# The delta rule of a hybrid layer: 16x16 substitution blocks with one more level of products, and the sample's chunk padded to 128 tokens

## The chip, the cores and the metric

The kernel runs on one core of a Trainium2 chip. The metric is the device time of one execution in microseconds (us). The core has five engines that work side by side, each on a queue of its own that it runs in order: PE (TensorE, matrix products), DVE (VectorE), ACT (ScalarE), POOL (GpSimd) and SP (SyncE), which here only issues DMA transfers. An engine whose next instruction waits for a semaphore does nothing that is queued behind it.

## What is computed

One layer of a streaming encoder: a projection of the normed input, then two branches, a gated delta rule over 16 heads and a sparse attention, then two output projections. There are 512 prompt tokens and 64 sample tokens (T = 576). The change is in the delta rule. Cut to what matters, for each head:

```
A  = where(strict, (k * beta) @ k.T * decay, 0)          # within a chunk
Tm = triangular_solve(eye + A, eye)                       # inverse of a unit lower triangle
u, w = Tm @ (v * beta), Tm @ (k * beta * exp(gc))
qk = (q @ k.T) * decay
def step(S, ...):                                         # one chunk after the other
    v_new = u_i - w_i @ S
    o_i   = qd_i @ S + qk_i @ v_new
    S     = S * g_last + kd_i.T @ v_new
```

The kernel takes chunks of 128 tokens for the prompt (chunks 0 to 3) and one of 64 for the sample (chunk 4), which starts from a state of its own.

## The kernel before

**The stream.** All projections run as one stream of products `mm` on PE: 128 weight columns against 288 tokens, weights and input split in a high and a low part, so that a tile of 128 columns takes 3 x 16 x 2 = 96 products. `half` issues them, `split` makes the two parts of the next tile's weights (`whi`, `wlo`), `load` fetches raw weights (`wraw`) on SP's queue. A head of the delta rule has about four and a quarter tiles of the stream beside it: its q, k and v columns, and others that it shares the stage with.

**The planner.** Everything else is a set of generator tasks. After each stream product `tick` steps the tasks that are due. A task yields what it waits for; the planner (class `Plan`) keeps its own estimate of when each buffer is ready, with fixed costs for each engine and for DMAs, and a task is due when that estimate says so. So the order of every engine's queue is fixed when the program is built, by estimates; on the chip semaphores make each instruction wait for what it really needs. `take` and `drop` are locks: only one head at a time is in `solve` (the lock "solve"), and only one in `scan`.

**A head.** `conv` makes q, k and v; `decays` the two decay matrices `QK` and `N` (tiles named e1 and e2, `e` in the trace). `front_k` multiplies k with itself (`within`, products kk, the sample's part apart as kk6s in head 6), scales `N` and starts `solve`; `front_q` does the same for q (kq). `tokens` turns k and v into token order (`kd`, `vb`).

**solve** inverts the unit lower triangles of the five chunks. It stores `N` to DRAM (`dN`), gathers the 18 diagonal blocks of 32x32 into `M`, one block a partition, and runs 30 substitution steps of two DVE operations each (a product into `Mt`, a sum into `M`). A transposed copy `X` goes beside it. Both are stored (`dX`) and loaded back by ten transfers to the diagonal blocks of `TT` (the transposed inverse) and `T1`. Products then join blocks: z0 and z1 from 32 to 64, y0 and y1 from 64 to 128:

```
self.mm(o, N[R, at:at + 32], TT[R, at + 32:at + 64], tile_position=(b + 32, b))                  # z0
self.mm(o, T1[b:b + 32, 64 * t:64 * t + 32], Z[b:b + 32, t, :], tile_position=(b, b))             # z1
```

**scan** takes the chunks in the order 0, 1, 4, 2, 3. In each: `pks` = K S and `po` = Q S on PE, `r` on DVE, `px` = TT r on PE, `x` on ACT, `pS` = kd x and `po` += QK x on PE, the new `S` on DVE. For the sample all of these are 64 tokens wide. At the end `oTp` and `oTq` transpose the head's output. All operations but those of PE are recorded by one helper, so they have one line in the profile (L55); the stream and the small products have L218, the transposes L233.

## Time and profile before

| | us |
|---|---|
| median of three runs | 3089.07 |
| the three runs | 3082.39, 3091.2, 3089.07 |
| the profiled execution | 3076.14 |
| its span | 3074.4 |
| PE busy | 2949.8 (96%) |
| DVE busy | 1389.5 (45%) |
| ACT busy | 1542.1 (50%) |
| POOL busy | 390.6 (13%) |

The profiled execution is one more run of the same kernel, recorded by the hardware; all rows below are from it. Its time is a little above its span, which goes from the first recorded instruction to the last. Busy time of PE counts overlapping products once. The 16 heads of the delta rule lie between about 560 and 1640 us of the span.

### The profile page before, as it was taken

The page shows a single profiled execution, that of the slowest core. Times are in us where ns is not written, and L with a number is a line of the kernel's source. Part 1 is how long each engine was busy: PE and PEld are TensorE (multiplying, and loading weights), DVE is VectorE, ACT ScalarE, POOL GpSimd, SP SyncE. Part 2 cuts the span into 40 slices and gives each one's busy share as a digit, 9 for nine tenths or more (in the row PEclk, how much of TensorE's full clock was granted, in tenths as well). Part 3 has the DMA queues.
Part 4 walks back from the last instruction along what each step waited for, and adds up shares of the span by engine and source line. Part 5 has one row for each costly group of instructions (what it writes and reads, how often), then busy time and mean ns, then how long its engine had stood idle before and what let it go on. Part 6 is the DMA issues. An engine that isn't in the chain of part 4 may idle for free.

```text
span 3074.4 us, 56422 instructions
## 1 busy us (share of the span) xinstructions
PE 2949.8 (96%) x22363; PEld 2811.9 (91%) x22363; DVE 1389.5 (45%) x4059; ACT 1542.1 (50%) x3332; POOL 390.6 (13%) x727
## 2 busy tenths in 40 slices
PE   6999999999999999999998799999999999999897
PEld 2599999999999989999997799899999999999897
DVE  3344997666567657666641344344412111111112
ACT  3266445565555556665553355445544444444454
POOL 1001111111111111111110011011111111111110
PEclk7999999999999999999998899999999999999999
DMA  9865887766666666677667767776769899888875
GB/s 327 279 157 124 196 184 178 159 154 155 142 149 145 151 146 148 148 172 161 156 151 155 163 167 171 188 171 160 174 152 250 220 240 237 215 203 223 215 161 140
DMA packets 567242, 552.40 MB, mean 180 GB/s; under 512 B 53505, under 2 KB 466066, under 8 KB 565762
## 3 DMA queue, kind: packets, MB, share of 16 engines
q1 hardware_dynamic: 512690, 351.58, 40.5%
q0 software_dynamic: 54144, 197.16, 33.7%
q8 instruction: 176, 2.88, 0.4%
q14 instruction: 88, 0.72, 0.1%
q10 hardware_dynamic: 144, 0.07, 0.0%
HBM read 303.54 MB, written 48.04 MB: 114 GB/s over the span
## 4 chain that ended last, share of the span: by engine, by line
PE 78%; DMA 11%; SPq 3%; ACT 3%; DVE 3%; issue 2%; POOL 0%; ACTq 0%; DVEq 0%; POOLq 0%
PE mm L218 63%; SPq L55 3%; DMA za<-d_za 2%; DMA wlo<-wraw 2%; DMA gbl<-d_gb 1%; PE ada L218 1%; PE ob L218 1%; DMA wa<-in_w_ada 1%; PE lg L218 1%; PE po L218 1%; PE dot L218 1%; ACT wlo L55 1%; PE mmp L218 1%; DMA xf<-in_x_sample 1%; ACT whi L55 1%
## 5 line engine op out<-in xcount | busy, mean ns | idle before, releaser
L218 PE MATMUL mm<-hh,whi 128*128 128x288 f32 (+1 forms) x4448 | 1221.0, 301 | 4.5 <-ACT gth L55 4.2
L218 PE MATMUL mm<-hl,whi 128*128 128x288 f32 (+1 forms) x4448 | 1218.3, 300 | 0.0
L218 PEld LDWEIGHTS mm<-hh,whi 128*128 128x128 f32 (+1 forms) x4448 | 839.6, 189 | 18.1 <-issue 7.8
L218 PEld LDWEIGHTS mm<-hl,whi 128*128 128x128 f32 (+1 forms) x4448 | 840.1, 189 | 10.2 <-issue 6.1
L218 PE MATMUL mm<-hh,wlo 128*128 128x288 f32 (+1 forms) x4448 | 682.5, 303 | 4.8 <-DMA wlo<-wraw 4.8
L218 PEld LDWEIGHTS mm<-hh,wlo 128*128 128x128 f32 (+1 forms) x4448 | 618.2, 191 | 11.5 <-DMA wlo<-wraw 5.1
L55 POOL DMA_DIRECT2D wlo<-wraw x376 | 324.5, 863 | 2311.4 <-ACT wlo L55 2035.2
L55 ACT ACTIVATE wlo<-whi 128x512 fp32r<-128x512 f32 x752 | 475.8, 633 | 81.1 <-PE mm L218 46.1
L55 ACT ACTIVATE whi<-wraw 128x512 fp32r<-128x512 f32 x756 | 467.9, 619 | 78.4 <-DMA wraw<-in_w_branch_b 27.5
L55 DVE TENSOR_TENSOR Mt<-M 18x30 f32<-18x30 f32 (+14 forms) x480 | 151.7, 316 | 31.2 <-DMA M<-dN 21.9
L55 DVE TENSOR_TENSOR M<-M,Mt 18x30 f32<-18x30 f32 (+14 forms) x480 | 153.6, 320 | 16.7 <-DVE Mt L55 0.3
L218 PE MATMUL mm<-ga,whi 128*128 128x288 f32 x1024 | 140.9, 297 | 6.1 <-DVE ta L55 5.0
L218 PE MATMUL mm<-mg,whi 128*128 128x288 f32 x1024 | 144.9, 299 | 0.0
L218 PEld LDWEIGHTS mm<-ga,whi 128*128 128x128 f32 x1024 | 138.2, 190 | 7.0 <-DVE ta L55 5.7
L218 PEld LDWEIGHTS mm<-mg,whi 128*128 128x128 f32 x1024 | 139.5, 190 | 0.0
L218 PE MATMUL mm<-gb,whi 128*128 128x288 f32 x1024 | 138.6, 295 | 0.0
L218 PEld LDWEIGHTS mm<-gb,whi 128*128 128x128 f32 x1024 | 136.8, 188 | 0.0
L55 DVE SCALAR_TENSOR_TENSOR cv<-raw,cw,cv 128x579 f32<-128x579 f32 x144 | 117.4, 815 | 4.3 <-ACT cv L55 0.8
L55 DVE SCALAR_TENSOR_TENSOR gacc<-gada,cs,gacc 128x512 f32<-128x512 f32 x120 | 86.7, 745 | 31.4 <-DMA gada<-in_w_ada 31.4
L55 ACT ACTIVATE x<-px 128x128 f32<-128x128 f32 (+1 forms) x80 | 22.0, 275 | 149.2 <-PE px L218 149.2
L55 ACT ACTIVATE raw<-mm 128x288 f32<-128x288 f32 x96 | 36.7, 382 | 99.0 <-PE mm L218 98.2
L55 DVE TENSOR_TENSOR xf<-yp,xf 128x512 f32<-128x512 f32 (+1 forms) x18 | 11.4, 633 | 161.9 <-PE yp L233 134.8
(478 smaller groups left out, 3298.7 us busy)
## 6 DMA issues: line engine op xcount, KB each, us to landing
wlo<-wraw POOLq DMA_DIRECT2D x376, 512.0 KB, 5.4
wraw<-in_w_in SPq DMA_DIRECT2D x140, 1024.0 KB
wa<-in_w_ada SPq DMA_DIRECT2D x64, 512.0 KB
gada<-in_w_ada SPq DMA_DIRECT2D x64, 256.0 KB
wraw<-in_w_branch_a SPq DMA_DIRECT2D x16, 1024.0 KB
wraw<-in_w_branch_b SPq DMA_DIRECT2D x16, 1024.0 KB
wraw<-in_w_out SPq DMA_DIRECT2D x16, 1024.0 KB
d_t<-gth SPq DMA_DIRECT2D x32, 288.0 KB
```

Source lines behind the costliest of these rows:

```text
L55: r = f(*a, **k)
L218: self.nc.tensor.matmul(out, lhsT, rhs, start=start, stop=stop, **k)
```

## The change

The diagonal blocks become 16x16: 36 of them in `M`, 14 substitution steps instead of 30, five gathers instead of six. `M` and `X` go to two DRAM tiles `d_D0` and `d_D1`, which are filled with zeros once before the first head; ten transfers write the blocks to their places on the diagonal (`blocks`), and two transfers load the whole tiles, `d_D1` into `TT` and `d_D0` into a new tile `Df`. Two new stages of products, u0 and u1, join blocks from 16 to 32: 18 and 31 products of 32x32, each on the diagonal 32x32 tile of PE that belongs to its partitions, with a mask `ur` in between that keeps the upper right quarter. Then z0, z1, y0 and y1 follow as before.

For the sample's chunk, q, k, kd, vb, TT and e1 get 64 further columns or rows of zeros, so that its products are 128 wide; the outputs of the added tokens are not stored. The memsets for that are on POOL. All lines behind the new ones move: L55, L218 and L233 become L58, L221 and L236.

The diff, cut to its core:

```
--- before.py
+++ after.py
...
+TXP = 643
+TC = 640
...
+        self.d_D = [dt([128, T], F32, name=f"d_D{e}") for e in range(2)]
...
-            dst = st["qk"[j]] = p.tile([128, TX], F32, tag="qk"[j], name="qk"[j] + str(h))
+            full = st["qk"[j]] = p.tile([128, TXP], F32, tag="qk"[j], name="qk"[j] + str(h))
+            G.memset(full[:, TX:], 0.0)
+            dst = full[:, :TX]
...
+        self.G.memset(dst[64:128, 4, :], 0.0)
...
-        e1 = p.tile([128, T], F32, tag="e1", name=f"e1{h}")
+        e1x = p.tile([128, TC], F32, tag="e1", name=f"e1{h}")
+        G.memset(e1x[:, T:], 0.0)
+        e1 = e1x[:, :T]
...
-            self.mm(pk[:, b:b + n] if c < 4 else ps[:n, :n], k[:, a:a + n], x[:, a:a + n])
+            self.mm(pk[:, b:b + n] if c < 4 else ps[:, :n], k[:, a:a + 128], x[:, a:a + n])
...
+    def blocks(self, d, t):
+
+        return bass.AP(tensor=d.tensor, offset=d.offset + 128 * t, ap=[[16 * T + 16, 8 if t < 4 else 4], [T, 16], [1, 16]])
+
     def solve(self, st):
 
 
         A, V, G, S, p, h, N = self.A, self.V, self.G, self.S, self.p2, st["h"], st["N"]
         if h > 1:
             yield from self.wait(self.heads[h - 2]["scan"])
-        TT = p.tile([128, T], F32, tag="TT", name=f"TT{h}")
+        TTX = p.tile([128, TC], F32, tag="TT", name=f"TT{h}")
+        TT = TTX[:, :T]
+        G.memset(TTX[:64, T:], 0.0)
+        G.memset(TTX[64:128, TP:], 0.0)
         T1 = p.tile([128, 288], F32, tag="T1", name=f"T1{h}")
         N4, TT4, T4 = by_chunk(N), by_chunk(TT), T1[:, :256].rearrange("p (a b) -> p a b", b=64)
-        for x in (TT4[32:64, :, 0:32], TT4[64:128, :, 0:64], TT4[96:128, :, 64:96], TT[32:64, TP:TP + 32], T4[0:32, :, 32:64]):
-            G.memset(x, 0.0)
+        G.memset(T4[0:32, :, 32:64], 0.0)
         yield from self.take("solve")
         yield [N]
         dN = self.dp.tile([128, T], F32, tag="dN", name=f"dN{h}", bufs=2)
         S.dma_start(dN, N)
         yield [dN]
-        MX = p.tile([128, 32, 32], F32, tag="M", name=f"M{h}", bufs=1)
-        M, X = MX[0:18], MX[64:82]
+        MX = p.tile([128, 16, 16], F32, tag="M", name=f"M{h}", bufs=1)
+        M, X = MX[0:36], MX[64:100]
+        for t in range(5):
+            S.dma_start(M[8 * t:min(8 * t + 8, 36)], self.blocks(dN, t))
+        yield [MX]
+        tmp = p.tile([36, 64], F32, tag="Mt", name=f"Mt{h}", bufs=1)
+        for j in range(1, 15):
+            n = 15 - j
+            w = [36, n, j]
+            tv = tmp[:, :n * j].rearrange("p (a b) -> p a b", b=j)
+            V.tensor_tensor(tv, M[:, j + 1:16, j:j + 1].to_broadcast(w), M[:, j:j + 1, 0:j].to_broadcast(w), op=ALU.mult)
+            V.tensor_tensor(M[:, j + 1:16, 0:j], M[:, j + 1:16, 0:j], tv, op=ALU.add)
+            yield ("dve", self.solve_gap)
+        V.memset(M.rearrange("p a b -> p (a b)")[:, 0:256:17], 1.0)
+        A.activation(X, M.rearrange("p a b -> p b a"), AF.Copy)
+        yield [MX]
+
+        for e, x in enumerate((M, X)):
+            for t in range(5):
+                S.dma_start(self.blocks(self.d_D[e], t), x[8 * t:min(8 * t + 8, 36)])
+        yield [self.d_D[0], self.d_D[1]]
+        Df = p.tile([128, T], F32, tag="Df", name=f"Df{h}", bufs=1)
+        S.dma_start(TT, self.d_D[1])
+        S.dma_start(Df, self.d_D[0])
+        D4 = by_chunk(Df)
         B = [slice(32 * b, 32 * b + 32) for b in range(4)]
-        C = [slice(TP + 32 * b, TP + 32 * b + 32) for b in range(2)]
-        for b in range(4):
-            S.dma_start(M[4 * b:4 * b + 4], by_chunk(dN)[B[b], :, B[b]].rearrange("r t c -> t r c"))
-        for b in range(2):
-            S.dma_start(M[16 + b:17 + b], dN[B[b], C[b]].unsqueeze(0))
-        yield [MX]
-        tmp = p.tile([18, 256], F32, tag="Mt", name=f"Mt{h}", bufs=1)
-        for j in range(1, 31):
-            n = 31 - j
-            w = [18, n, j]
-            tv = tmp[:, :n * j].rearrange("p (a b) -> p a b", b=j)
-            V.tensor_tensor(tv, M[:, j + 1:32, j:j + 1].to_broadcast(w), M[:, j:j + 1, 0:j].to_broadcast(w), op=ALU.mult)
-            V.tensor_tensor(M[:, j + 1:32, 0:j], M[:, j + 1:32, 0:j], tv, op=ALU.add)
-            yield ("dve", self.solve_gap)
-        V.memset(M.rearrange("p a b -> p (a b)")[:, 0:1024:33], 1.0)
-        A.activation(X, M.rearrange("p a b -> p b a"), AF.Copy)
-        dX = self.dp.tile([2, 18, 32, 32], F32, tag="dX", name=f"dX{h}", bufs=2)
-        yield [MX]
-        S.dma_start(dX[0], M)
-        S.dma_start(dX[1], X)
-        yield [dX]
-        for b in range(4):
-            S.dma_start(TT4[B[b], :, B[b]], dX[1, 4 * b:4 * b + 4].rearrange("t r c -> r t c"))
-            if b < 3:
-                S.dma_start(T4[B[b], :, B[b % 2]], dX[0, 4 * b:4 * b + 4].rearrange("t r c -> r t c"))
-        for b in range(2):
-            S.dma_start(TT[B[b], C[b]], dX[1, 16 + b])
-        S.dma_start(T1[0:32, 256:288], dX[0, 16])
-        yield [TT, T1], 3000.0
+        blk = [(t, g) for t in range(5) for g in range(4 if t < 4 else 2)]
+        yield [TT, Df], 3000.0
 
         Z = p.tile([128, 5, 32], F32, tag="Z", name=f"Z{h}", bufs=1)
+        pz = yield from self.tr(f"u0{h}")
+        for t, g in blk:
+            at = slice(128 * t + 32 * g, 128 * t + 32 * g + 32)
+            self.mm(pz[B[g], 32 * t:32 * t + 32], N[B[g], at], TT[B[g], at], tile_position=(32 * g, 32 * g))
+        V.tensor_tensor(Z[:, 0:4, :], pz[:, 0:128].rearrange("p (a b) -> p a b", b=32),
+                        self.ur.unsqueeze(1).to_broadcast([128, 4, 32]), op=ALU.mult)
+        V.tensor_tensor(Z[0:64, 4, :], pz[0:64, 128:160], self.ur[0:64], op=ALU.mult)
+        yield [Z], 300.0
+        pz = yield from self.tr(f"u1{h}")
+        for t, g in blk:
+            at = slice(128 * t + 32 * g, 128 * t + 32 * g + 32)
+            self.mm(pz[B[g], 32 * t:32 * t + 32], Df[B[g], at], Z[B[g], t, :], tile_position=(32 * g, 32 * g))
+            if g < (3 if t < 4 else 1):
+                self.mm(pz[B[g], 160 + 32 * t:192 + 32 * t], Z[B[g], t, :], Df[B[g], at], tile_position=(32 * g, 32 * g))
+        for g in range(4):
+            R, c = slice(32 * g, 32 * g + 16), 32 * g + 16
+            A.activation(TT4[R, :, c:c + 16], pz[R, 0:128].rearrange("p (a b) -> p a b", b=32)[:, :, 16:32], AF.Copy)
+            if g < 2:
+                A.activation(TT[R, TP + c:TP + c + 16], pz[R, 144:160], AF.Copy)
+            if g < 3:
+                V.tensor_tensor(T4[B[g], :, B[g % 2]], pz[B[g], 160:288].rearrange("p (a b) -> p a b", b=32), D4[B[g], :, B[g]], op=ALU.add)
+        V.tensor_tensor(T1[0:32, 256:288], pz[0:32, 288:320], Df[0:32, TP:TP + 32], op=ALU.add)
+        yield [TT, T1], 300.0
+
         for step in range(2):
...
-        Y = p.tile([64, 256], F32, tag="Y", name=f"Y{h}", bufs=1)
+        Y = p.tile([64, 256], F32, tag="Mt", name=f"Y{h}", bufs=1)
...
-        st["TT"] = TT
+        st["TT"] = TTX
...
-                self.mm(pc[:n, :128], K[:, a:a + n], Sc)
-                self.mm(po[:n, :128], Q[:, a:a + n], Sc, stop=False)
+                self.mm(pc[:, :128], K[:, a:a + 128], Sc)
+                self.mm(po[:, :128], Q[:, a:a + 128], Sc, stop=False)
                 r = p.tile([128, 128], F32, tag="r", name=f"r{h}{c}", bufs=1)
-                V.scalar_tensor_tensor(r[:n], pc[:n, :128], wr[:n, c:c + 1], vb[:n, c, :], op0=ALU.mult, op1=ALU.add)
+                V.scalar_tensor_tensor(r, pc[:, :128], wr[:, c:c + 1], vb[:, c, :], op0=ALU.mult, op1=ALU.add)
                 yield [r], 100.0
-                r = r[:n]
             else:
-                r = vb[:n, c, :]
+                r = vb[:, c, :]
             px = yield from self.tp(f"px{h}{c}")
-            self.mm(px[:n, :128], TT[:n, b:b + n], r)
+            self.mm(px[:, :128], TT[:, b:b + 128], r)
             x = p.tile([128, 128], F32, tag="x", name=f"x{h}{c}")
-            A.activation(x[:n], px[:n, :128], AF.Copy)
+            A.activation(x, px[:, :128], AF.Copy)
             yield [x], 100.0
             pS = yield from self.tp(f"pS{h}{c}")
-            self.mm(pS[:, :128], kd[:n, c, :], x[:n])
-            self.mm(po[:n, :128], QK[:n, b:b + n], x[:n], start=Sc is None)
+            self.mm(pS[:, :128], kd[:, c, :], x)
+            self.mm(po[:, :128], QK[:, b:b + 128], x, start=Sc is None)
             Sn = p.tile([128, 128], F32, tag="S", name=f"S{h}{c}", bufs=3)
             if Sc is not None:
                 V.scalar_tensor_tensor(Sn, Sc, st["gl"][:, c:c + 1], pS[:, :128], op0=ALU.mult, op1=ALU.add)
             else:
                 V.tensor_copy(Sn, pS[:, :128])
-            A.activation(ot[:n, c, :], po[:n, :128], AF.Copy)
+            A.activation(ot[:, c, :], po[:, :128], AF.Copy)
...
-            n = 128 if t < 4 else 64
-            A.activation(ot[:n, t, :], ot[:n, t, :], AF.Copy, scale=s[:n, t:t + 1])
+            A.activation(ot[:, t, :], ot[:, t, :], AF.Copy, scale=s[:, t:t + 1])
-        self.T32(pt[:, :64], ot[:64, 4, :])
+        self.T32(pt[:, :128], ot[:, 4, :])
...
+        zero = self.p2.tile([128, T], F32, tag="Df", name="zero", bufs=1)
+        self.G.memset(zero, 0.0)
+        for d in self.d_D:
+            self.S.dma_start(d, zero)
...
+    c["k_ur"] = ((p % 32 < 16) & (f[:, :32] >= 16)).astype(np.float32)
```

**The order of the instructions.** Numbers in names are of the head and then of the buffer: `M5` is of head 5, `S54` of head 5 and chunk 4, `pks42` of head 4 and chunk 2. Shapes are partitions x elements of the output.

DVE before, where the substitution of head 5 begins. The first row is the state of head 4 behind chunk 1; the last is the `r` of its sample chunk.

```order
L55 SCALAR_TENSOR_TENSOR S41_9338<-S40_9261,egl4_8604,pS41_0_9335 128x128
L55 TENSOR_TENSOR Mt5_9361<-M5_9319 18x30
L55 TENSOR_TENSOR M5_9319<-M5_9319,Mt5_9361 18x30
L55 TENSOR_TENSOR Mt5_9361<-M5_9319 18x58
L55 TENSOR_TENSOR M5_9319<-M5_9319,Mt5_9361 18x29x2
L55 SCALAR_TENSOR_TENSOR r44_9374<-pks44_0_9371,sc4_8155,vb4_8901 64x128
```

DVE in the changed kernel, at the same place of head 5: the state of head 4 behind chunk 2 now stands behind two steps of substitution, and what stands ahead is its `r`.

```order
L58 SCALAR_TENSOR_TENSOR r42_9438<-pks42_0_9435,sc4_8244,vb4_9102 128x128
L58 TENSOR_TENSOR Mt5_9454<-M5_9417 36x14
L58 TENSOR_TENSOR M5_9417<-M5_9417,Mt5_9454 36x14
L58 TENSOR_TENSOR Mt5_9454<-M5_9417 36x26
L58 TENSOR_TENSOR M5_9417<-M5_9417,Mt5_9454 36x13x2
L58 SCALAR_TENSOR_TENSOR S42_9471<-S41_9267,egl4_8878,pS42_0_9468 128x128
```

The first substitution operations have moved from behind chunk 1 of the scan of head 4 to behind the `r` of its chunk 2, and a state `S` instead of an `r` is the first scan operation behind them.

DVE in the changed kernel, where the substitution of head 6 begins, between the state of head 5 behind its sample chunk and the `r` of its chunk 2.

```order
L58 SCALAR_TENSOR_TENSOR S54_10365<-S05_10149,egl5_9773,pS54_0_10362 128x128
L58 TENSOR_TENSOR Mt6_10376<-M6_10334 36x14
L58 TENSOR_TENSOR M6_10334<-M6_10334,Mt6_10376 36x14
L58 TENSOR_TENSOR Mt6_10376<-M6_10334 36x26
L58 TENSOR_TENSOR M6_10334<-M6_10334,Mt6_10376 36x13x2
L58 SCALAR_TENSOR_TENSOR r52_10391<-pks52_0_10388,sc5_9306,vb5_9954 128x128
```

Here too the scan of the head before has its next operation right behind the first four of the substitution.

SP before, from the state that the scan of head 4 needs to the stores of head 5's solved blocks; ten loads into `TT5` and `T15` follow a little later.

```order
L55 DMA S04_9235<-in_state_gdn 128x128
L55 DMA dN5_9237<-e25_8947 128x576
L55 DMA M5_9319<-dN5_9237 4x32x32 x4
L55 DMA M5_9319<-dN5_9237 1x32x32 x2
L55 DMA out_new_gdn_sample<-S44_9407 128x128
L55 DMA wraw50_9445<-in_w_in 128x16x128
L55 DMA out_new_gdn_prompt<-S43_9596 128x128
L55 DMA wraw51_9674<-in_w_in 128x16x128
L55 DMA d_oa_82<-oT4_9634 128x576
L55 DMA gB6_9873<-d_g_79 128x579
L55 DMA wraw52_9878<-in_w_in 128x16x128
L55 DMA dX5_9852<-M5_9319 18x1024 x2
```

SP in the changed kernel, from the store of head 5's `N` to the first of the two loads that bring the blocks home (the load of `Df5` is next).

```order
L58 DMA dN5_9376<-e25_9023 128x576
L58 DMA M5_9417<-dN5_9376 8x16x16 x4
L58 DMA M5_9417<-dN5_9376 4x16x16
L58 DMA out_new_gdn_sample<-S44_9413 128x128
L58 DMA wraw49_9479<-in_w_in 128x16x128
L58 DMA out_new_gdn_prompt<-S43_9540 128x128
L58 DMA d_D0_88<-M5_9417 8x16x16 x4
L58 DMA d_D0_88<-M5_9417 4x16x16
L58 DMA d_D1_89<-M5_9417 8x16x16 x4
L58 DMA d_D1_89<-M5_9417 4x16x16
L58 DMA wraw50_9692<-in_w_in 128x16x128
L58 DMA TT5_9319<-d_D1_89 128x576
```

Between gathers and stores of the blocks stood two outputs, three weight loads, the store of a head's output and the load of a row of decays; now there are two outputs and one weight load. Two stores have become ten, and ten loads two.

## Rows read from the trace of the kernel before

**Rows 1.** The page: span and instruction count.

```profile
span 3074.4 us, 56422 instructions
```

**Rows 2.** Stretches: PE, PEld, DVE, ACT, POOL busy; PE clock, DMA share, GB/s.

```profile
560.00:1617.00 1057.00, 1037.66 (x8452) 994.83 (x8451) 681.39 (x2283) 611.73 (x1373) 159.73 (x422) 0.99 0.67 154
838.40:848.60 10.20, 7.23 (x27) 6.07 (x28) 3.99 (x15) 1.53 (x4) 0.00 (x0) 0.50 0.15 32
1128.50:1138.80 10.30, 9.21 (x35) 7.71 (x36) 4.67 (x17) 1.53 (x4) 0.00 (x0) 0.50 0.35 92
1637.10:1643.90 6.80, 6.76 (x27) 5.79 (x27) 0.57 (x2) 6.30 (x13) 0.86 (x1) 0.50 0.40 96
```

**Rows 3.** Groups by line and shape, 560 to 1660: busy, mean ns; idle before.

```profile
L233 PE MATMUL oTp<-ident,ot 128*128 128x128 f32 x64 | 10.3, 282 | 3.7 <-ACT ot L55 3.7
...
L218 PE MATMUL z<-TT,e 32*32 32x32 f32 x270 | 10.3, 197 | 8.6 <-DMA TT<-dX 3.3 <-DVE rkt L55 2.4 <-DVE sc L55 1.9
...
L218 PE MATMUL px<-r,TT 64*64 64x128 f32 x30 | 6.9, 314 | 10.7 <-DVE r L55 10.7
...
L55 DVE TENSOR_TENSOR Mt<-M 18x58 f32<-18x58 f32 x29 | 6.0, 207 | 1.0
```

**Rows 4.** Timeline of PE in head 5: start, duration, [idle before].

```profile
841.37 0.68 PE L218 MATMUL px<-r,TT 64*64 64x128 f32 x2 [4.66 <-DVE r L55]
```

**Rows 5.** Timeline of DVE in head 5.

```profile
840.15 0.19 DVE L55 TENSOR_TENSOR Mt<-M 18x30 f32<-18x30 f32 x1 [7.88 <-DMA M<-dN]
```

**Rows 6.** Timeline of DVE in head 13.

```profile
1411.63 0.19 DVE L55 TENSOR_TENSOR Mt<-M 18x30 f32<-18x30 f32 x1 [5.03 <-DMA M<-dN]
```

**Rows 7.** Timeline of PE around the kk products of head 6.

```profile
887.91 0.29 PE L218 MATMUL mm<-hh,whi 128*128 128x288 f32 x1
888.04 1.05 PE L218 MATMUL kk<-k 128*128 128x128 f32 x8
...
889.52 0.29 PE L218 MATMUL mm<-hh,whi 128*128 128x288 f32 x1
889.65 0.30 PE L218 MATMUL mm<-hl,whi 128*128 128x288 f32 x1
```

**Rows 8.** Timeline of PE, head 15: products around z1, sample px, sample pS, next px.

```profile
1600.65 0.29 PE L218 MATMUL mm<-hl,whi 128*128 128x288 f32 x1
...
1601.54 0.29 PE L218 MATMUL mm<-hl,whi 128*128 128x288 f32 x1
...
1617.09 0.29 PE L218 MATMUL mm<-hl,whi 128*128 128x288 f32 x1
...
1617.91 0.29 PE L218 MATMUL mm<-hl,whi 128*128 128x288 f32 x1
...
1619.90 0.29 PE L218 MATMUL mm<-hh,whi 128*128 128x288 f32 x1
...
1621.14 0.29 PE L218 MATMUL mm<-hh,whi 128*128 128x288 f32 x1
...
1623.71 0.29 PE L218 MATMUL mm<-hh,whi 128*128 128x288 f32 x1
...
1624.20 0.29 PE L218 MATMUL mm<-hh,whi 128*128 128x288 f32 x1
```

**Rows 9.** Timeline of DVE in head 6: the last operation on e.

```profile
895.04 0.24 DVE L55 TENSOR_SCALAR e<-e,sc 64x64 f32<-64x64 f32 x1
```

**Rows 10.** Timeline of SP in head 6: issues of DMAs.

```profile
897.48 0.55 SPq L55 DMA_DIRECT2D dN<-e  x1
902.10 3.32 SPq L55 DMA_DIRECT2D M<-dN  x6
```

**Rows 11.** Timeline of SP in head 5.

```profile
826.49 0.38 SPq L55 DMA_DIRECT2D dN<-e  x1
831.06 5.60 SPq L55 DMA_DIRECT2D M<-dN  x6
```

**Rows 12.** Timeline of SP in head 13.

```profile
1404.23 3.44 SPq L55 DMA_DIRECT2D M<-dN  x6
```

More of the change, by code (lines that the diff above doesn't have):

```diff
@@ L475, in start @@
             S.dma_start(self.diag, i["k_diag"])
+            S.dma_start(self.ur, i["k_ur"])
             def load_x(t):
@@ L989, in decays @@
         A.activation(gB, gB, AF.Exp)
-        st.update(QK=e1, N=e2)
+        st.update(QK=e1, QKX=e1x, N=e2)
     def within(self, name, k, x, dst):
@@ L1037, in front_q @@
         sq = p.tile([128, TX], F32, tag="th", name=f"sq{h}", bufs=1)
-        A.activation(sq, Q, AF.Square)
+        A.activation(sq, Q[:, :TX], AF.Square)
         yield from self.within(f"kq{h}", K, Q, QK)
@@ L1051, in front_q @@
         eg = st["gB"]
-        V.tensor_tensor(Q, Q, eg, op=ALU.mult)
+        V.tensor_tensor(Q[:, :TX], Q[:, :TX], eg, op=ALU.mult)
         gl = st["gl"] = p.tile([128, 5], F32, tag="egl", name=f"egl{h}")
@@ L1149, in scan @@
             yield 200
-        K, Q, QK, TT, kd, vb, wr = (st[n] for n in ("k", "q", "QK", "TT", "kd", "vb", "wr"))
+        K, Q, QK, TT, kd, vb, wr = (st[n] for n in ("k", "q", "QKX", "TT", "kd", "vb", "wr"))
         yield from self.take("scan")
@@ L1799, in run @@
             self.diag = cp.tile([128, 64], F32, name="diag")
+            self.ur = cp.tile([128, 32], F32, name="ur")
             self.heads, self.att, self.kvT, self.tok = {}, {}, {}, {}
```

## Prediction

> **What bounds the kernel now.** I read the views in this order: the page, the busy table by stretches, the groups by line and shape, and then the timelines of PE, DVE and SP around three heads. The profiled execution took 3076.14 us, 1.7 more than its span [rows 1]; the median of the other three runs is 3089.07. My sum is made on the 3076.14, and the difference of 12.9 is added at the end.
>
> The sixteen heads lie between 560 and about 1640 us. There PE is busy 1037.7 of 1057 us at a granted clock of 0.99 [rows 2], while DVE has 681 us of work, ACT 612 and POOL 160. So in this stage TensorE's time counts, and other engines matter only where PE waits for them. The whole idle time of PE that touches this change is in four rows: z waits 8.6 us in all, the 64x64 px 10.7, all of it for r, and the last head's oTp 3.7 [rows 3].
>
> The px wait is the one to understand. In head 5, px stands 4.66 us because DVE has not made r [rows 4]. DVE itself stood 7.88 us at the first substitution product, Mt 18x30, until the blocks M had been gathered, and r is queued four instructions behind it [rows 5]. DVE runs its queue in order, so a substitution that is issued before its gather has landed holds up the scan of the head before. The order ahead shows it: Mt, M, Mt, M, then r. The same stands in head 13 (5.03 us, [rows 6]). Most other heads don't have it: there the solve lock of the head before keeps Mt late. Behind such a wait PE is granted 0.50 for 10.2 us; after the oTp wait for 6.8 us [rows 2].
>
> **PE's own work.** I price a small group as the start of the second stream product behind it, less the start of the last one ahead, less two spacings of 0.13 [rows 7]. That takes in the cost of leaving and entering a tile shape.
> - Padding. The sample chunk's 64x64 px costs 1617.91 − 1617.09 − 0.26 = 0.56; the 128x128 px 1624.20 − 1623.71 − 0.26 = 0.23; so 0.33 less. The sample's pS with po costs 1621.14 − 1619.90 − 0.26 = 0.98 [rows 8]; two full ones at 0.23 are 0.46, 0.52 less. pks with po, oTq and the sample parts of kk (the whole group 1.35, [rows 7]) and kq are four more shape changes that go; each I put at a little under px's 0.33, in all 1.25. Sum 2.1 us a head, 34 us in 16 heads. It could be as little as px and pS alone, 0.85 x 16 = 14.
> - u0 and u1. z1, 13 products of 32x32 of which one tile holds five, costs 1601.54 − 1600.65 − 0.26 = 0.63 [rows 8]. u0 has 18 on four diagonal tiles, again at most five on one: 0.65. u1 has 31, up to ten on one tile: with half of z1's price for entering and leaving and half for five products, 0.31 + 2 x 0.31 = 0.93 at least; were all 31 in a row at 0.06, 2.2. I take 1.1, near the low end, since z1's row shows tiles working side by side. 1.75 x 16 = 28 us (25 to 46).
> - Net: −6 us (−9 to +32).
>
> Half the substitution steps go: 28 DVE operations instead of 60, none larger than the 18x58 one of 0.207 us [rows 3]. DVE isn't the bound, so this gives nothing directly; POOL's four extra memsets a head and the two products by the mask hide behind engines that stand more than a third of this stage; a POOL or DVE piece at the end of a solve would show as idle time of PE at u1 or z, with its own length. What the fewer steps do is make the solve shorter, by 32 operations of at least 0.2 us, over 6 us in DVE alone, and that moves the next solve.
>
> A rule of the Trainium skill speaks against the padding: TensorEngine Tiling, Theoretical Speedup, gives up to 2x where a dimension is at most 64. By that rule the padded products would cost an estimated 10 us in all instead of saving 34. The rows disagree (0.56 for the half-size px, 0.23 for the full one).
>
> **The wait at the first substitution.** With solves shorter, the lock is free when the next one asks for it, and the planner issues Mt as soon as it believes that M is there. How late is M really? Counted from the start of the kk products in head 6: the masked e is ready 7.2 us later (888.04 to 895.28, [rows 7, 9]); dN is through SP up to 2.8 after that [rows 10] where a wraw and a state load stand ahead on SP, and I take 1; the gather starts 4.6 behind the issue of dN (897.48 to 902.10 and 826.49 to 831.06, [rows 10, 11]); and from the first gather to M landed were 9.1 us in head 5 (831.06 to 840.15, [rows 5, 11]) and 7.4 in head 13 (1404.23 to 1411.63, [rows 6, 12]). Five gathers instead of six, with the same 576 rows half as long: I take 6.5. Bounds: only the issue of five, 2.8, and the 9.1 that was. M lands at kk + 19 (15 to 24).
>
> Where does DVE reach Mt? I counted the stream products between the kk group and the scan's product whose result DVE reads just ahead of Mt in the new order: 76 in head 5 to pks42, 86 in head 6 to pS54; at 0.13, with 2 to 4 us of the scan's own products between them, kk + 12.5 to kk + 16. Twelve of sixteen heads are like this; heads 0, 1, 3 and 9 have Mt at a place where nothing urgent is behind. So DVE stands 3 to 6.5 us in twelve heads. Behind it r or S comes at once (order ahead), and PE's next px or pks waits: in head 5 of before a stand of 7.88 became 4.66 for PE. I take 3 us of PE a head, 36 us.
>
> The clock: the stand of 4.66 was followed by 10.2 us at 0.50, the one of 3.7 by 6.8 [rows 2], each losing half of that. For 3 us I take 1.5 lost (bounds 0 and 5.1), 18 us. Together +54. The same products are where the old waits were, so these go: 10.7 for px and two spells of 10.2 at half clock (the other was in head 9), in all −21.
>
> **The way back.** M goes out by ten scatters and comes home by two loads; before it was two stores and ten loads. Ten issues at the gathers' 0.55 [rows 10] are 5.5 us, landing and load at most 4.6 each [rows 10, 11]: 11 to 15 us, and the transposed copy ahead of it. Between the memset and u0 the new order has about 120 stream products, 16 to 18.5 us with what lies between. So I cost it at nothing, and the 8.6 us of z waits go as well, since z now comes behind u1. If the cover is short, each head pays.
>
> **The tail.** Head 15's scan ends earlier against the next stage, so the 3.7 us of oTp and part of the spell behind it go: −5.
>
> Sum: 54 − 21 − 8.6 − 5 − 6 = +13; on 3076.1 that is 3089.5, on the median's footing 3102.
>
> **Rivals.**
> 1. M is there in time. If it lands by kk + 16, or the planner places Mt later than I counted, there is no new wait and the sum is −21 − 8.6 − 5 − 6 = −41: 3048. For it: only two or three heads of before show such a stand, and the gathers are smaller. Against: all rows of the gather's way give more than 16. Chance 0.28.
> 2. The way back is late. 64-byte rows scattered into DRAM, both ways over one queue; if u0 waits 2 us a head and loses 1 to the clock, +48 on the forecast: about 3150. Against: the 120 products. No row of before has a scatter of this kind. Chance 0.10. The Trainium skill's DMA: Bandwidth & Descriptors, Specifications, says that transfers under 512 B are read, changed and written back; no run here shows it yet.
> 3. u1's products don't run side by side: 2.2 instead of 1.1, +18: 3121. For it: two of its kinds share a tile. Against: z1. Chance 0.07.
> 4. Padding gives nothing, because the price of 0.56 is a price of the place and a full-size group there would pay it too: +34, 3137. Against: the same place has both sizes three microseconds apart. Chance 0.03. The Trainium skill's TensorEngine Tiling would end near here too.
> 5. Waits are moved to where others hide them, and what is won pays for what is lost: 3089. Chance 0.05.
>
> **How the numbers follow.** The forecast has 0.47, with a range of its own of 3085 to 3145 from 2 to 5 us in twelve heads. Of 3089, 0.3% is 9.3 us, about what a measurement of this kernel can tell from no change. Faster: rival 1 and a little of the forecast's low end, 0.29. Same: rival 5 and the lower part of the forecast's own range, 0.16. Slower: the rest, 0.55. The range 3050 to 3150 leaves out rival 1's lower half and the worst of rival 2.
>
> **What the changed profile would show.** Right: the 36x14 Mt waits on M in about twelve heads with several us each; the sample's px, now 128x128, or pks idle for r or S; the clock at 0.50 behind it; u0 with no idle time; pS with po near 0.46. Wrong: Mt finds M there (rival 1), u0's idle row is tens of us (rival 2), or u1 takes over 2 us (rival 3).

## The result, and the profile after

The changed kernel takes 3064.21 us (median of four runs, 3058.79 to 3069.4) against 3085.78 of before: a ratio of 0.9929, interval 0.9913 to 0.9945. A second measurement on another occasion gave 0.9918 (0.9900 to 0.9936). It is 22 to 25 us faster; the forecast was 13 us slower than the median of that time. The mechanism is that of rival 1 (M is there in time), but with half of its gain. Two things are to be explained: why the wait at the substitution stayed away, and where the other half of the 41 us went.

The page of the changed kernel: span and busy time of PE and DVE (execution time 3063.92).

```profile
span 3061.8 us, 59253 instructions
...
PE 2934.6 (96%) x23931; PEld 2814.4 (92%) x23931; DVE 1204.6 (39%) x3643; ACT 1533.3 (50%) x3428; POOL 391.5 (13%) x776
```

The head stage, columns as in [rows 2].

```profile
560.00:1617.00 1057.00, 1040.80 (x10031) 1012.62 (x10029) 513.04 (x1900) 616.38 (x1488) 163.25 (x469) 1.00 0.70 161
```

The same 1057 us hold more work in the changed kernel: PE has 1600 more instructions, 91 of them products of the stream, and is busy 3 us more; DVE works 168 us less. The groups by line and shape over the same stretch as [rows 3]:

```profile
L221 PE MATMUL px<-r,TT 128*128 128x128 f32 x120 | 24.0, 282 | 0.1
L221 PE MATMUL pks<-S,k 128*128 128x128 f32 x120 | 23.5, 277 | 0.6 <-DVE S L58 0.5
...
L58 ACT ACTIVATE TT<-u 16x64 f32<-16x64 f32 x60 | 12.8, 213 | 32.7 <-DVE T L58 18.7 <-PE u L221 14.0
L58 DVE TENSOR_TENSOR T<-u,Df 32x128 f32<-32x128 f32 x45 | 12.8, 283 | 31.0 <-ACT TT L58 31.0
L221 PE MATMUL u<-Z,Df 32*32 32x32 f32 x540 | 11.9, 197 | 1.8 <-DVE Z L58 1.1 <-DMA Df<-d_D 0.7
...
L236 PE MATMUL oTp<-ident,ot 128*128 128x128 f32 x64 | 9.6, 272 | 0.0
...
L236 PE MATMUL vbp<-ident,raw 128*128 128x128 f32 x60 | 9.4, 279 | 1.3 <-ACT kd L58 1.3
...
L221 PE MATMUL u<-TT,e 32*32 32x32 f32 x540 | 7.8, 194 | 0.9 <-DMA TT<-d_D 0.9
L221 PE MATMUL z<-TT,e 32*32 32x32 f32 x270 | 7.5, 194 | 0.0
...
L58 DVE TENSOR_TENSOR Mt<-M 36x14 f32<-36x14 f32 x28 | 4.7, 167 | 20.5 <-DMA M<-dN 20.1
...
L236 PE MATMUL kdq<-ident,k 128*64 128x128 f32 x15 | 4.2, 277 | 5.5 <-DVE T L58 4.4 <-ACT kd L58 1.1
L236 PE MATMUL vbq<-ident,raw 128*64 128x128 f32 x15 | 4.1, 273 | 2.8 <-DVE T L58 2.5
...
L236 PE MATMUL nc<-ident,newc 128*96 128x128 f32 x2 | 0.6, 292 | 3.5 <-DVE ncr L58 3.5
```

Read against [rows 3]: px waited 10.7 us, now 0.1, and pks 0.6; z waited 8.6, now 0.0; oTp 3.7, now 0.0. So all the old waits that the prediction counted as gone are gone. DVE does stand at the first Mt, 20.1 us in all, but PE doesn't lose it. And there are waits that the prediction doesn't have: kdq 5.5, vbq 2.8, vbp 1.3, y 1.8 (two rows of the same view, left out here), u 2.7, and nc 3.5 at the end of the stage, in the place of oTp. The two rows on TT<-u and T<-u are the ones to look at: ScalarE's copies of u1's result stood 18.7 us for VectorE's sums, and VectorE's sums 31.0 us for ScalarE's copies. Neither engine reads what the other has written.

The whole of the heads' work, from the first kk product to the last oTq, in the kernel before and in the changed one (columns as in [rows 2]):

```profile
438.80:1638.40 1199.60, 1176.54 (x9546) 1128.81 (x9544) 776.93 (x2545) 685.04 (x1523) 181.31 (x473) 0.99 0.68 155
```

```profile
440.00:1602.70 1162.70, 1146.50 (x10990) 1116.70 (x10989) 592.09 (x2129) 670.99 (x1607) 180.76 (x517) 1.00 0.70 161
```

PE stood 23.1 us before and stands 16.2 now. The stage is 36.9 us shorter, but 124 products of the stream that it held before, 16 us at 0.13, come behind it now; what is left, 21 us, is the gain. Of it 7 us are idle time, about 12 are the lower clock of before, and PE's own work is the same within 2 us.

The price of u1 by the same reckoning as in the prediction, from the stream products around it in head 9:

```profile
1143.17 0.29 PE L221 MATMUL mm<-hl,whi 128*128 128x288 f32 x1
...
1144.38 0.29 PE L221 MATMUL mm<-hl,whi 128*128 128x288 f32 x1
```

1144.38 − 1143.17 − 0.26 = 0.95.

### The profile page after: what moved, and what is told of

Its sections match the earlier page's. It is cut to its first block, busy times and chain, and to the rows that moved or that the text cites. A ratio compares the mean times of both kernels' runs of the same rounds, so it can differ in the third digit from the quotient of the medians.

```text
span 3061.8 us, 59253 instructions
## 1 busy us (share of the span) xinstructions
PE 2934.6 (96%) x23931; PEld 2814.4 (92%) x23931; DVE 1204.6 (39%) x3643; ACT 1533.3 (50%) x3428; POOL 391.5 (13%) x776
## 4 chain that ended last, share of the span: by engine, by line
PE 82%; DMA 9%; DVE 3%; ACT 3%; SPq 2%; issue 1%; POOL 0%; ACTq 0%; DVEq 0%; POOLq 0%
PE mm L221 67%; SPq L58 2%; DMA za<-d_za 1%; DMA wlo<-wraw 1%; PE ada L221 1%; PE ob L221 1%; DMA gbl<-d_gb 1%; PE lg L221 1%; PE mmp L221 1%; PE dot L221 1%; PE po L221 1%; DMA xf<-in_x_sample 1%; DMA wa<-in_w_ada 1%; ACT whi L58 1%; ACT wlo L58 1%
## 5 line engine op out<-in xcount | busy, mean ns | idle before, releaser
L221 PE MATMUL mm<-hh,whi 128*128 128x288 f32 (+1 forms) x4448 | 1217.2, 300 | 4.8 <-ACT gth L58 4.5
L221 PE MATMUL mm<-hl,whi 128*128 128x288 f32 (+1 forms) x4448 | 1215.9, 300 | 0.0
L221 PEld LDWEIGHTS mm<-hh,whi 128*128 128x128 f32 (+1 forms) x4448 | 837.8, 188 | 14.0 <-ACT gth L58 5.3
L221 PEld LDWEIGHTS mm<-hl,whi 128*128 128x128 f32 (+1 forms) x4448 | 837.8, 188 | 7.9 <-issue 3.8
L221 PE MATMUL mm<-hh,wlo 128*128 128x288 f32 (+1 forms) x4448 | 683.0, 302 | 4.5 <-DMA wlo<-wraw 4.5
L221 PEld LDWEIGHTS mm<-hh,wlo 128*128 128x128 f32 (+1 forms) x4448 | 615.6, 190 | 6.6 <-DMA wlo<-wraw 4.7
L58 POOL DMA_DIRECT2D wlo<-wraw x376 | 324.0, 862 | 2313.2 <-ACT wlo L58 1926.8
L58 ACT ACTIVATE whi<-wraw 128x512 fp32r<-128x512 f32 x756 | 467.4, 619 | 98.1 <-DMA wraw<-in_w_branch_b 63.1
L58 ACT ACTIVATE wlo<-whi 128x512 fp32r<-128x512 f32 x752 | 475.2, 632 | 76.4 <-PE mm L221 35.9
L221 PE MATMUL mm<-ga,whi 128*128 128x288 f32 x1024 | 142.4, 299 | 7.5 <-DVE ta L58 7.5
L221 PEld LDWEIGHTS mm<-ga,whi 128*128 128x128 f32 x1024 | 139.7, 192 | 8.4 <-DVE ta L58 8.4
L221 PE MATMUL mm<-mg,whi 128*128 128x288 f32 x1024 | 143.6, 297 | 0.0
L221 PE MATMUL mm<-gb,whi 128*128 128x288 f32 x1024 | 138.8, 296 | 0.3 <-DVE tb L58 0.3
L221 PEld LDWEIGHTS mm<-mg,whi 128*128 128x128 f32 x1024 | 138.2, 189 | 0.0
L221 PEld LDWEIGHTS mm<-gb,whi 128*128 128x128 f32 x1024 | 136.8, 188 | 0.6 <-DVE tb L58 0.5
L58 DVE SCALAR_TENSOR_TENSOR cv<-raw,cw,cv 128x579 f32<-128x579 f32 x144 | 117.8, 818 | 33.6 <-ACT cv L58 30.4
L58 DVE SCALAR_TENSOR_TENSOR gacc<-gada,cs,gacc 128x512 f32<-128x512 f32 x120 | 86.7, 744 | 30.9 <-DMA gada<-in_w_ada 30.8
L58 ACT ACTIVATE raw<-mm 128x288 f32<-128x288 f32 x96 | 36.8, 383 | 87.4 <-PE mm L221 86.6
L58 ACT ACTIVATE gth<-mm 128x288 f32<-128x288 f32 x64 | 25.9, 407 | 108.3 <-PE mm L221 104.6
L58 ACT ACTIVATE x<-px 128x128 f32<-128x128 f32 x80 | 22.0, 275 | 116.0 <-PE px L221 115.6
L58 DVE TENSOR_TENSOR xf<-yp,xf 128x512 f32<-128x512 f32 (+1 forms) x18 | 11.4, 632 | 160.5 <-PE yp L236 133.7
L58 DVE SCALAR_TENSOR_TENSOR tb<-tb,mm 128x288 f32<-128x288 f32 x32 | 14.5, 452 | 143.3 <-DMA tb<-d_t 110.3
```

The lines of the kernel that those rows point to most:

```text
L58: r = f(*a, **k)
L221: self.nc.tensor.matmul(out, lhsT, rhs, start=start, stop=stop, **k)
```

## The experiments

Fourteen runs, two of them repeats; medians, with ratios to the kernel before on the same chip.

| kernel | median us | ratio | interval |
|---|---|---|---|
| pad_alone | 3081.49 | 0.9984 | 0.9971 to 0.9997 |
| blocks_alone | 3091.42 | 1.0020 | 1.0007 to 1.0034 |
| late_m2 | 3098.65 | 1.0041 | 1.0025 to 1.0057 |
| late_m3 | 3132.26 | 1.0148 | 1.0133 to 1.0162 |
| late_m8 | 3268.05 | 1.0593 | 1.0569 to 1.0617 |
| late_m16 | 3470.40 | 1.1240 | 1.1216 to 1.1264 |
| mt_slack4 | 3081.17 | 0.9992 | 0.9978 to 1.0005 |
| u1_two_banks | 3043.41 | 0.9861 | 0.9845 to 0.9876 |
| two_banks_again | 3045.99 | 0.9872 | 0.9852 to 0.9893 |
| u1_grouped | 3057.61 | 0.9911 | 0.9897 to 0.9926 |
| u1_dve | 3061.63 | 0.9933 | 0.9911 to 0.9955 |
| u1_other_bank | 3054.64 | 0.9898 | 0.9876 to 0.9919 |
| blocks_two_banks | 3081.79 | 0.9995 | 0.9985 to 1.0006 |
| after_again | 3060.23 | 0.9918 | 0.9900 to 0.9936 |

**The two parts alone.** pad_alone is the changed kernel with the solve of before, its TT and Y in the new places; blocks_alone is the kernel before with the new solve.

> The sample's chunk padded to 128, the 32x32 substitution as before (Y shares the place of Mt, for room). If the prices of the prediction hold and the two parts of the change add up, TensorE's own work falls by 2.1 us a head, 34 us, the solve's waits stay as they were, and the time is about 3052 against 3086 of before, faster than the whole change (3064). Rival: with less work for TensorE beside it the long solve becomes late, and the waits for r and for the home load of TT take back half or more: 3068 to 3085.

> 16x16 blocks with u0 and u1, the sample's chunk 64 wide as before. If the parts add up: 26 us of new products on TensorE (0.65 + 0.95 a head), the old waits for r and TT gone (19 us idle and 10 us of clock), the tail's 4 us gone, new waits of about 20 us at kdq, vbq, u and the tail: within 10 us of before, 3080 to 3100. Rival: the blocks are what made the change faster: 3064 or less. Rival: the u1 stage is more than it looks, over 3105.

Padding alone gives 5 us, inside the range of its rival; the blocks alone cost 6, as expected; both together give 22 to 25: the parts don't add up. In pad_alone, the groups of PE:

```profile
L221 PE MATMUL px<-r,TT 128*128 128x128 f32 x124 | 25.4, 287 | 9.2 <-DVE r L58 9.2
...
L221 PE MATMUL z<-TT,e 32*32 32x32 f32 x270 | 12.5, 202 | 28.7 <-DMA TT<-dX 20.7 <-DVE dg L58 2.8 <-DVE rkt L58 2.6
```

z, which waits for the loads home, stands 28.7 us instead of 8.6, and px still 9.2. From the first kk to the last oTq PE stands 41.6 us instead of 23.1, and the granted clock is 0.98 instead of 0.99. The work that the padding takes from PE was the cover of the long solve, so most of it comes back as waits and lower clock: the rival that was given for this run. The blocks alone shorten the solve and take old waits away (PE stands 12.9 us instead of 23.1, at a clock of 1.00), and about as much goes into the two new stages of products. Each part makes room for the other.

**M later.** The changed kernel with extra gathers between the fourth and the fifth; the planner doesn't see them, so that no other engine's order changes.

```
+        M2 = p.tile([128, T], F32, tag="Df", ...)[:8, :256].rearrange("p (a b) -> p a b", b=16)
         for t in range(5):
+            if t == 4:
+                for _ in range(8):                       # 16, 2, 3
+                    S.eng.dma_start(M2, self.blocks(dN, 0))
             S.dma_start(M[8 * t:min(8 * t + 8, 36)], self.blocks(dN, t))
```

> The changed kernel with eight more gathers into an unused place between the fourth gather and the fifth, not shown to the planner: M lands about 2.8 us later (at 0.35 us each), and nothing else moves on TensorE, VectorE, ScalarE or GpSimd. So M lands at the time the prediction took, 19 us behind kk. If the prediction's price of a stand of VectorE was right (3 us of TensorE and 1.5 of clock in twelve heads for a stand of 3 to 6.5 us), this costs about 50 us: 3115. Rival: the first 2.5 us or so of a stand are free, since TensorE's next product of the scan is that far off; then six or seven heads lose 1 to 3 us: 3070 to 3085. Rival: stands are hidden altogether: 3064.

> As late_m8 with sixteen, M about 5.6 us later: VectorE stands 5.5 to 8.5 us in twelve heads. By the prediction's price: 6 us of TensorE and 3 of clock a head, 110 us: 3170. Rival with the first 2.5 us free: 3 to 6 us of TensorE in twelve heads and up to half a spell of 5 to 10 us at half clock behind each: 3120 to 3150. Hidden altogether: 3064.

Both were far over every figure, for a reason that the timeline of SP shows in head 5 of late_m8:

```profile
889.69 11.46 SPq L1097 DMA_DIRECT2D M<-dN  x8
```

Eight gathers into one place take 11.46 us, 1.43 each: in the trace each waits for the semaphore of the one before it, since they write the same place. The dose was 11.5 us (and 23), not 2.8. The cost is of that size: 204 us over sixteen heads is 12.7 a head for a delay of 11.5. The smaller doses were set by this.

> As late_m8 with two extra gathers. There the extra gathers went out one after another, 1.43 us each (11.46 us for eight), not 0.35, so that run was a delay of 11.5 us and not of 2.8. Two should make M late by 1.9 us. VectorE then stands 2 us in the heads where r is next and 5 us where S is next; if TensorE loses the stand less 1.1 (r) and less 2.5 (S), as late_m8 shows for long stands, that is about 1 and 2.4 us a head, 22 us, and 5 to 13 of clock: 3085 to 3100. Rival: short stands cost nothing: 3064 to 3070.

> Three extra gathers, M late by 3.5 us: it lands 18 to 20 us behind kk, which is the time that the prediction took (19). If the prediction was wrong only in that time, its price comes back: +54 on 3064, 3118, with 3105 to 3135 as bounds. If it was also wrong in the price of a stand: below 3095 (short stands are hidden) or above 3140 (the half clock weighs more).

Both came out inside their ranges, late_m3 14 us over its centre. In late_m3 the groups of PE and DVE, and head 11: the stand of DVE, the product of the scan behind it, and the stretch after that (columns as in [rows 2]):

```profile
L221 PE MATMUL px<-r,TT 128*128 128x128 f32 x120 | 26.0, 300 | 15.0 <-DVE r L58 14.9
...
L221 PE MATMUL pks<-S,k 128*128 128x128 f32 x118 | 24.2, 287 | 20.2 <-DVE S L58 20.2
...
L221 PE MATMUL u<-TT,e 32*32 32x32 f32 x540 | 8.1, 198 | 8.7 <-DMA TT<-d_D 8.7
...
L58 DVE TENSOR_TENSOR Mt<-M 36x14 f32<-36x14 f32 x28 | 4.7, 167 | 70.7 <-DMA M<-dN 70.3
```

```profile
1294.03 0.17 DVE L58 TENSOR_TENSOR Mt<-M 36x14 f32<-36x14 f32 x1 [6.58 <-DMA M<-dN]
```

```profile
1295.14 0.80 PE L221 MATMUL pks<-S,k 128*128 128x128 f32 x2 [3.77 <-DVE S L58]
```

```profile
1295.10:1299.00 3.90, 3.86 (x17) 3.86 (x18) 2.50 (x13) 0.53 (x2) 0.00 (x0) 0.50 0.93 253
```

DVE stands 6.58 us, S is made four operations later, and pks loses 3.77; behind it the granted clock is 0.50 for 3.9 us and more. Summed, px and pks stand 15.0 + 20.2 = 35.2 us, in twelve heads, all but 0, 1, 3 and 9. The prediction's figure for M at this time was 36, in the same twelve. What it doesn't have is u, which now stands 8.7 us for the load home (0.9 in the changed kernel): the solve ends later, and its way back is no longer covered.

**No stand at all.** The planner is told that M comes 4 us later than it reckons.

```
-        yield [MX]
+        yield [MX], 4000.0
```

> The changed kernel, but the planner takes M to be ready 4 us later than it reckoned, so that no VectorE stand at Mt is left. If the stands of up to 3 us that remain cost TensorE nothing, the time stays (3060 to 3068). If they cost something that the idle rows don't show, 3050 to 3058. Rival: the solve ends 4 us later and its home load isn't covered: 3070 or more.

```profile
L236 PE MATMUL vbp<-ident,raw 128*128 128x128 f32 x60 | 10.2, 295 | 10.9 <-DVE raw L58 10.9
...
L58 DVE TENSOR_TENSOR Mt<-M 36x14 f32<-36x14 f32 x29 | 4.8, 166 | 1.3 <-DMA M<-dN 0.6 <-issue 0.2
```

The stand is gone (1.3 instead of 20.5), and the time is 17 to 21 us longer than that of the changed kernel: the solve's later steps fall in another place, where vbp waits 10.9 us for a conv result. This is the third expectation in sign and size, though the home load has a small part of it (u stands 3.3 us for it instead of 0.9). With so much else moved, this run doesn't price the stands of the changed kernel; that they cost next to nothing is read from its own rows, px 0.1 and pks 0.6.

**The results of u1.** In u1_two_banks the second kind of products goes to a bank of its own.

```
         pz = yield from self.tr(f"u1{h}")
+        pw = yield from self.tp(f"u1w{h}")
...
-                self.mm(pz[B[g], 160 + 32 * t:192 + 32 * t], Z[B[g], t, :], Df[B[g], at], ...)
+                self.mm(pw[B[g], 32 * t:32 * t + 32], Z[B[g], t, :], Df[B[g], at], ...)
```

The reason for it, in head 11 of the changed kernel. DVE's four sums, ACT's six copies, and the first product of PE that needs the bank again:

```profile
1271.50 0.27 DVE L58 TENSOR_TENSOR T<-u,Df 32x128 f32<-32x128 f32 x1
1272.12 0.28 DVE L58 TENSOR_TENSOR T<-u,Df 32x128 f32<-32x128 f32 x1 [0.35 <-ACT TT L58]
1272.68 0.29 DVE L58 TENSOR_TENSOR T<-u,Df 32x128 f32<-32x128 f32 x1 [0.28 <-ACT TT L58]
1273.25 0.18 DVE L58 TENSOR_TENSOR T<-u,Df 32x32 f32<-32x32 f32 x1 [0.28 <-ACT TT L58]
```

```profile
1270.18 0.28 ACT L58 ACTIVATE TT<-u 16x64 f32<-16x64 f32 x2 [0.35 <-PE u L221]
1271.81 0.28 ACT L58 ACTIVATE TT<-u 16x64 f32<-16x64 f32 x2 [1.35 <-DVE T L58]
1272.43 0.21 ACT L58 ACTIVATE TT<-u 16x64 f32<-16x64 f32 x1 [0.35 <-DVE T L58]
1273.00 0.22 ACT L58 ACTIVATE TT<-u 16x64 f32<-16x64 f32 x1 [0.35 <-DVE T L58]
```

```profile
1273.58 0.27 PE L236 MATMUL kdq<-ident,k 128*64 128x128 f32 x1 [1.80 <-DVE T L58]
```

The engines take turns: copy, sum, copy, sum. While one works the other stands 0.28 to 0.35 us; the change itself, from the end of one to the start of the other, takes 0.03 to 0.04. From the first copy to the end of the last sum are 3.25 us (about 1.0 of them because the first sum stands behind other work of DVE), and kdq waits 1.80 for that bank. PE's wait for the bank, at kdq or vbq, is this long (1.75 to 1.80) in heads 5, 11 and 13, where the first sum was late in this way; in heads 14 and 15 it is 0.8. The sum over block row g and the copy for g + 1 touch other partitions, and still wait.

> The changed kernel with the two kinds of products of u1 in two banks, so that ScalarE's copies to TT and VectorE's sums to T1 read different tiles. In the changed kernel they take turns on the one tile, and TensorE waits 8 us in all for that tile at kdq and vbq. If this turn-taking is what makes those waits: 5 to 8 us less, 3056 to 3060. Rival: the second bank is one that pks and px use, so the wait moves there: 3064 or more. Rival: VectorE's queue, not the turns, makes T1 late: 3062 to 3066.

The same operations in the two-bank kernel, DVE and ACT, and its groups of PE:

```profile
1262.01 1.07 DVE L58 TENSOR_TENSOR T<-u1w,Df 32x128 f32<-32x128 f32 x4 [2.00 <-PE u1w L221]
```

```profile
1262.05 1.02 ACT L58 ACTIVATE TT<-u 16x64 f32<-16x64 f32 x6 [1.32 <-PE u1w L221]
```

```profile
L236 PE MATMUL vbp<-ident,raw 128*128 128x128 f32 x60 | 9.2, 276 | 0.0
...
L236 PE MATMUL vbq<-ident,raw 128*64 128x128 f32 x15 | 4.2, 279 | 0.1
L236 PE MATMUL kdq<-ident,k 128*64 128x128 f32 x15 | 4.1, 277 | 1.0 <-ACT kd L58 1.0
```

Both engines run at the same time, 1.1 us in all; kdq, vbq and vbp stand 1.1 us instead of 9.6. The time falls by 14 to 21 us (against both measurements of the changed kernel), more than the first expectation (5 to 8) and more than these three rows. The whole stage shows more of it:

```profile
439.60:1584.60 1145.00, 1142.33 (x10990) 1116.18 (x10988) 591.99 (x2129) 671.94 (x1607) 184.85 (x517) 1.00 0.71 164
```

With as many products as in the changed kernel it is 17.7 us shorter, and PE stands 2.7 us instead of 16.2: nearly all new waits are gone, those of y and u too.

> The two-bank kernel once more on the same chip: 3036 to 3048.

The next two keep one bank and take the turns away: u1_grouped puts all copies ahead of all sums, u1_dve makes the copies on VectorE.

```
         for g in range(4):                                # u1_grouped
             ...copies...
+        for g in range(4):
             ...sums...
-            A.activation(TT4[R, :, c:c + 16], ..., AF.Copy)   # u1_dve
+            V.tensor_copy(TT4[R, :, c:c + 16], ...)
```

> The changed kernel with one bank for u1, but ScalarE's six copies first and then VectorE's four sums. With two banks the kernel took 3043 against 3064, and TensorE's waits at kdq, vbq, vbp and y went from about 13 us to 1. If the turns are the cause, most of that comes back here with one change of engine instead of six: 3046 to 3054. If it is the second bank (the first one free sooner, or one more in all), this stays at 3060 to 3068.

> All ten readings of u1's bank on VectorE, so no change of engine at all. By the turns: 3045 to 3055, a little more if VectorE's longer queue (six more operations of about 0.2 us a head) is late for the scan. By the second bank: 3060 to 3068.

> The changed kernel once more, on the same chip as the other three: 3058 to 3070, for their comparison.

u1_grouped gains 3 us on after_again, which is inside the intervals, and u1_dve nothing. So turns alone don't make most of it. From u1's last product to the end of the last sum the traces have, as the median over the heads, 2.3 us in the changed kernel, 2.2 in u1_grouped, 2.15 in u1_dve and 1.1 with two banks: ten readings one after another take as long with one change of engine, or none, as with seven. A part of the waits does go with the turns: in u1_grouped PE stands 10.8 us from the first kk to the last oTq, 16.7 in after_again, since the copies no longer stand behind a late first sum. And u1_dve is no clean test: kdq, vbq, vbp and y stand 3.6 us there instead of 11.4, but z stands 9.5 for sums in VectorE's longer queue.

> The changed kernel with all of u1 in one bank, but in one of the two that pks, px and pS use, instead of one of the two that u0, z, y, kd, vb, kk and kq use. Readings of u1's result stay one after another (2.3 us behind its last product; with two banks 1.1). If what the two-bank kernel won came from the first pair of banks being asked for once less a head, the time is 3043 to 3050. If it came from the readings going side by side, the wait moves to pks and px or stays: 3055 to 3068.

```
-        pz = yield from self.tr(f"u1{h}")
+        pz = yield from self.tp(f"u1{h}")
```

```profile
L221 PE MATMUL px<-r,TT 128*128 128x128 f32 x120 | 24.5, 285 | 2.3 <-DVE r L58 2.2
...
L221 PE MATMUL u<-TT,e 32*32 32x32 f32 x540 | 8.0, 197 | 4.0 <-DMA TT<-d_D 4.0
...
L221 PE MATMUL z<-TT,e 32*32 32x32 f32 x270 | 7.8, 193 | 3.0 <-ACT TT L58 3.0
...
L236 PE MATMUL kdq<-ident,k 128*64 128x128 f32 x15 | 4.2, 283 | 0.3 <-ACT kd L58 0.3
```

3055, 6 to 10 us less than the changed kernel and some 9 more than with two banks. kdq doesn't wait any more (0.3), but px 2.3, z 3.0 and u 4.0 do (3.4 of u's in one head, for a load; the profiled execution is the slowest of the six). So both seem to have a part: that pair of banks was asked for too often, and the readings are too long. How the 14 to 21 us split between them stays open: moving the bank gave 6 to 10, and the intervals are some 6 us wide.

> The 16x16 blocks without the padding, u1 in two banks. Against blocks_alone (3091) the second bank should give the 20 us that it gave the whole change: 3068 to 3076. What is left to the padded two-bank kernel (3043) is then the padding's own part, 25 to 34 us by the prices of the prediction. If the padding's part is smaller here than that, the two parts do not simply add up even without the turns; if the second bank gives nothing here (3085 or more), the turns cost only where TensorE's stream is already short of cover.

Here the second bank gives 0.0025, 8 us, not 20: the expectation of 3068 to 3076 failed. Why less without the padding was not tried; blocks_alone has less to take away, since PE stands 12.9 us in it and 7.8 here. Padded and not, both with two banks, differ by 36 to 41 us. 7 of them are idle time and clock (PE stands 7.8 and 2.7 us), so the padding's own part is 29 to 34. It comes through only with the short solve, and in full only with the second bank.

## Why the prediction was wrong

**How late is M really: the step that failed.** The forecast has M at kk + 19, and from that 54 us of stands and lower clock; M came about 3 us sooner, and the stands cost PE 0.7 us. Head 13 of the changed kernel, from the kk products on PE to the issues on SP, the stand of DVE, and the scan's next product.

```profile
1372.59 1.06 PE L221 MATMUL kk<-k 128*128 128x128 f32 x8
```

```profile
1379.79 0.33 SPq L58 DMA_DIRECT2D dN<-e  x1
1384.22 2.94 SPq L58 DMA_DIRECT2D M<-dN  x5
```

```profile
1388.75 0.17 DVE L58 TENSOR_TENSOR Mt<-M 36x14 f32<-36x14 f32 x1 [3.02 <-DMA M<-dN]
...
1389.47 0.33 DVE L58 SCALAR_TENSOR_TENSOR S<-S,egl,pS 128x128 f32<-128x128 f32 x1
```

```profile
1389.86 0.49 PE L221 MATMUL pks<-S,k 128*128 128x128 f32 x2 [0.21 <-DVE S L58]
```

DVE was free 3.02 us before 1388.75, which is kk + 13.1: inside the 12.5 to 16 that were counted from the order. M came at kk + 16.2, not 19. The other heads agree: where DVE stood, M came at kk + 14.7 to 16.7, and DVE was free at kk + 12.8 to 16.1. Of the four terms, e ready at 7.2 held and so did 4.4 from dN to the first gather (4.6); dN went out at once (I had 1 us for a load ahead of it), and from the first gather to M were 4.5 us and not 6.5. That last term had been taken from heads 5 and 13 of before, 9.1 and 7.4 [rows 5, 6, 11, 12]. These are heads in which DVE stood, and it stood because M was late: I had read the duration from slow cases, as those show as long waits. Head 4 of before was there to be read:

```profile
756.89 2.65 SPq L55 DMA_DIRECT2D M<-dN  x6
```

```profile
761.14 0.19 DVE L55 TENSOR_TENSOR Mt<-M 18x30 f32<-18x30 f32 x1 [0.69 <-DMA M<-dN]
```

First gather to M in 4.25 us, with a stand of 0.69. With 4.3 in the sum M lands at kk + 17, and the stand is 1 to 4.5. How much of the 2 us is this choice of heads, and how much comes from five smaller gathers in place of six, no run separates: of the five heads of before in which DVE stood for M, the other four had 7.4 us or more.

**What a stand costs: held.** A stand of 7.88 of DVE had become 4.66 of PE [rows 4, 5]; here 3.02 become 0.21, in late_m3 6.58 become 3.77. Where S is next, the first 2.8 us or so are free; where r is next it is less (in head 2 of late_m3 3.96 become 2.53), but there the changed kernel's stands are 0.4 us at most. late_m3 as a whole puts M about where the prediction had it (kk + 17.7 to 20.5), and px and pks stand 35.2 us (36 forecast). The time is 68 to 72 us over the changed kernel (54 forecast). From the first kk to the last oTq PE stands 49 us more and the low clock takes some 22 (18 forecast): so most of the excess is other waits, u's for the load home above all, and a little is the clock. Inside the changed kernel 20.1 us of DVE's stands cost PE 0.7. So the forecast's term was nearly right as a function of M's time, and its argument was 3 us off, which is the width of what is free.

**PE's own work: held.** u1 0.95 (1.1 forecast), u0 0.65 by the same reckoning (0.65 forecast). Padding 29 to 34 us between the two-bank kernels (34 forecast), so rival 4 is out. In sum PE's own work is the same within 2 us where the forecast had 6 less. The Trainium skill's TensorEngine Tiling, Theoretical Speedup, gives up to 2x where a dimension is at most 64. These single products in a stream of full-size ones went the other way. The new products don't run one after another (rival 3).

**The way back: held.** u waits 0.9 for TT and 0.7 for Df in all, so rival 2 is out. The Trainium skill's DMA: Bandwidth & Descriptors, Specifications, has transfers under 512 B read, changed and written back. The 64-byte scatters land in time here; what they cost inside, no run shows.

**The old waits: held. The tail: no.** px, z and oTp gave their 23 us back, and the granted clock over the stage is 1.00 instead of 0.99. But nc stands 3.5 us where oTp had 3.7.

**What the sum left out.** This is the second step that failed, and it took the other half of rival 1's gain: u1 was priced by its products, and what follows them was put at nothing. Its result has ten readings, and they hold a bank that kdq, vbq and y ask for next. PE's new waits over the heads are 16.2 us, where the sum had none; with two banks they are 2.7, the time is 14 to 21 us less, and the kernel lies 40 to 43 us below before, where rival 1 had put it (41). The Trainium skill has the rule (PSUM — Partial Sum Buffer, PSUM bank collisions raise a hardware error): ScalarE and VectorE must not be in one bank and quadrant at the same time, readings included, and the compiler puts a dependency between them. By that page other quadrants of a bank are free; the program's order here is stricter, since the copy for g + 1 waits for the sum over g. Whether the chip would need that wait, no run shows.

## What to carry to other kernels

A transfer's duration read from the places where somebody waited long for it is that of the late ones; read also a place where the wait was short or none. A new stage of products is priced with the readings of its result and with what next wants the bank; where two engines read, give each a bank, and they run side by side (here 40 to 43 us below before, the fastest version of the study). Two changes to one path can be worth nothing alone and much together, when one frees the time that the other's wait would fill.
